# Seven block products in place of eight in a feed-forward part, as two phases through DRAM

## The chip, the cores and the metric

One core of one Trainium2 chip runs the whole program. The time is device time in microseconds; a kernel is run several times, and the median counts. The engines are TensorE (PE; its weight loads are PEld), VectorE (DVE), ScalarE (ACT), GpSimd (POOL) and SyncE (SP), which issues the DMAs. Each has its own queue of instructions, in an order that is fixed when the program is built.

## The reference

A trunk of two layers is run over 1024 latent tokens and 128 prompt tokens of width 1024. Each layer is norm, mixer (attention), gated residual, norm, feed-forward part, gated residual; the shifts, scales and gates come from a conditioning vector (one for the latent tokens, another for the prompt). The change is in the feed-forward part, of inner width D_FF = 2816 (22 tiles of 128):

```python
def conv_ffn(h, w_up, conv_w, conv_b, w_down):
    gate, val = jnp.split(h @ w_up, 2, axis=-1)
    gp = jnp.pad(gate, ((0, 0), (1, 1), (0, 0)))
    gate = gp[:, :-2] * conv_w[0] + gp[:, 1:-1] * conv_w[1] + gp[:, 2:] * conv_w[2] + conv_b
    return (jax.nn.silu(gate) * val) @ w_down
...
        x = x + g1 * o
        h = rmsnorm(x, W['g_ffn_norm'][l]) * (1 + sc2) + sh2
        x = x + g2 * conv_ffn(h, W['w_up'][l], W['conv_w'][l], W['conv_b'][l], W['w_down'][l])
```

## The kernel before

Features lie on partitions (8 tiles, KD), tokens in columns: 1152 tokens in 3 chunks of CW = 384, the last of which holds 256 latent tokens and the prompt. Every float32 operand is split into a high part (cast to fp32r on ACT) and a low part (the difference, on DVE): `split`, L82 and L83. A product is then three matmuls, high x high, high x low and low x high (`mm3`, L87 to L89). Each matmul loads its own 128x128 weights and streams the tokens of a chunk.

A layer ends with the output projection (`out_proj`: 8 output tiles x 3 chunks x 8 x 3 matmuls into `odps`, added to the residual stream x on DVE by `x_add`, L498; squares for the norm on ACT, L194, and summed on GpSimd, L195), the norm of each chunk (`norm_chunk`, which gives Hhi and Hlo), and `ffn`. For each of the 22 inner tiles f, `ffn` computes the gate (`fg`, 8 x 3 matmuls for each of 3 chunks), copies it out on ACT, does the width-3 convolution in three DVE operations (L581 to L583) and SiLU on ACT, computes the value (`fv`), multiplies and splits on DVE and ACT, and after every second f runs the down product of a finished pair (`fd`: 8 output tiles x 3 chunks x 2 x 3 matmuls, each group added to x at once, L498). The up and down weights of one load (128x1024, 512 KB) are split by one ACT and one DVE operation. x, the activations and the weights stay in SBUF; x is read from DRAM once, in layer 0.

In layer 0, the modulation of what comes later is computed behind this: in the output projection 8 column tiles on DVE (`mod_dve`, L115) and 8 on GpSimd and ACT (`mod_pool`, L132 and L133), in the feed-forward part 56 on DVE, in pieces of 512 columns, queued behind a convolution (`held`). GpSimd has almost nothing to do in the feed-forward part.

The code states dependencies only through tiles. A planner lays the instructions of each engine in order by the times that it assumes for them, so that instructions which are ready go ahead of earlier ones which wait; on the chip each engine then keeps that order. The code before and after is planned in the same way.

## Time and profile before

| what | value |
|---|---|
| runs | 3173.3 us median of 3 (3172.89 to 3174.28) |
| profiled execution, first to last instruction | 3174.0 us |
| PE busy | 3069.4 us (97%), 18557 matmuls |
| DVE busy | 2149.7 us (68%) |
| ACT busy | 1307.4 us (41%) |
| GpSimd busy | 817.8 us (26%) |
| DMA | 163.96 MB, mean 52 GB/s |

Matmuls are pipelined, so that PE's busy time doesn't tell how near it is to its limit; the distance between the starts of successive matmuls does. The recorded duration of a DVE operation holds some 0.08 us that overlaps the next one, so that the distance of starts is the better price there too.

### The profile page before, as it was taken

Reading aid. Unit: us, or ns where it says so; the run is one execution under the profiler, and the core shown is the slowest. Engines: PE = TensorE matmul, PEld = TensorE weight load, DVE = VectorE, ACT = ScalarE, POOL = GpSimd, SP = SyncE. Lnnn points to the kernel's source line nnn. Section 1 sums busy time; section 2 is a strip of 40 time slices with the busy share of each in tenths; the row PEclk is TensorE's granted clock in tenths of the full one; section 3 lists DMA queues with packets and bytes.
Section 4 is the critical chain, followed back from the end, with each engine's and each line's share of the span. In section 5 each row is a group of like instructions: output and inputs, shape, how many; then the busy total and the mean of one; then the engine's idle time right before and its main releaser. Section 6 shows DMA issues by size and latency. Waiting matters only on the chain.

```text
span 3174.0 us, 49141 instructions
## 1 busy us (share of the span) xinstructions
PE 3069.4 (97%) x18557; PEld 2936.0 (93%) x18557; DVE 2149.7 (68%) x4980; ACT 1307.4 (41%) x2608; POOL 817.8 (26%) x970
## 2 busy tenths in 40 slices
PE   8889999999979999999999998999999999999998
PEld 6778998889879999999999987988999999999997
DVE  6668997888778867776754766989364454444446
ACT  4428886777634121221111425998241211211112
POOL 4336762434272000000000404987220000000003
PEclk8989999999989999999999998999999999999999
DMA  6200000000332322222211110001110111111111
GB/s 227 73 21 1 1 14 14 5 3 15 128 132 71 117 86 87 80 88 87 85 47 40 34 40 13 2 2 34 34 47 34 42 50 43 40 47 40 41 40 60
DMA packets 63407, 163.96 MB, mean 52 GB/s; under 512 B 6481, under 2 KB 18529, under 8 KB 62913
## 3 DMA queue, kind: packets, MB, share of 16 engines
q1 hardware_dynamic: 62994, 160.41, 14.7%
q8 instruction: 146, 2.39, 0.3%
q14 instruction: 91, 0.75, 0.1%
q0 software_dynamic: 176, 0.41, 0.0%
HBM read 155.67 MB, written 5.13 MB: 51 GB/s over the span
## 4 chain that ended last, share of the span: by engine, by line
PE 83%; DVE 8%; ACT 3%; issue 3%; POOL 2%; DMA 2%; SPq 0%; DVEq 0%; ACTq 0%; POOLq 0%
PE sps L326 8%; PE fg L88 6%; PE fg L87 6%; PE fg L89 6%; PE fv L87 6%; PE fv L88 6%; PE fv L89 6%; PE fd L89 6%; PE fd L87 6%; PE ptps L371 6%; PE fd L88 6%; PE pvps L392 3%; PE pvps L391 3%; PE ips L87 1%; PE ips L89 1%
## 5 line engine op out<-in xcount | busy, mean ns | idle before, releaser
L498 DVE SCALAR_TENSOR_TENSOR x<-fd,mod,x 128x384 f32<-128x384 f32 (+1 forms) x704 | 345.2, 513 | 537.5 <-PE fd L89 536.3
L195 POOL TENSOR_TENSOR nacc<-nacc,nsq 128x384 f32<-128x384 f32 x75 | 90.3, 1205 | 1688.6 <-ACT nsq L194 1686.4
L82 ACT CAST whi<-wraw 128x1024 fp32r<-128x1024 f32 (+2 forms) x184 | 180.2, 981 | 521.3 <-PE fg L88 248.8
L89 PE MATMUL fd<-ahi,wlo 128*128 128x384 f32 x1056 | 357.0, 338 | 0.0
L88 PE MATMUL fd<-alo,whi 128*128 128x384 f32 x1056 | 355.2, 336 | 0.0
L87 PE MATMUL fd<-ahi,whi 128*128 128x384 f32 x1056 | 354.5, 337 | 0.3 <-DVE x L498 0.3
L87 PE MATMUL fg<-Hhi,whi 128*128 128x384 f32 x1056 | 354.0, 335 | 0.0
L88 PE MATMUL fg<-Hlo,whi 128*128 128x384 f32 x1056 | 354.0, 336 | 0.0
L89 PE MATMUL fg<-Hhi,wlo 128*128 128x384 f32 x1056 | 353.9, 335 | 0.0
L87 PE MATMUL fv<-Hhi,whi 128*128 128x384 f32 x1056 | 353.8, 335 | 0.0
L88 PE MATMUL fv<-Hlo,whi 128*128 128x384 f32 x1056 | 353.7, 335 | 0.0
L89 PE MATMUL fv<-Hhi,wlo 128*128 128x384 f32 x1056 | 353.5, 335 | 0.0
L315 POOL TENSOR_SCALAR prob<-prob,pm 128x1280 f32<-128x1280 f32 (+3 forms) x288 | 283.9, 994 | 211.9 <-DVE pm L348 191.9
L371 PE MATMUL ptps<-cst,prob 128*128 128x128 f32 x1920 | 293.7, 274 | 4.1 <-POOL prob L315 2.6
L83 DVE TENSOR_TENSOR wlo<-wraw,whi 128x1024 fp32r<-128x1024 f32 (+2 forms) x184 | 215.9, 1176 | 105.1 <-ACT whi L82 104.9
L83 DVE TENSOR_TENSOR ptlo<-ptps,pthi 128x512 fp32r<-128x512 f32 (+1 forms) x428 | 273.7, 654 | 12.8 <-ACT pthi L82 8.7
L82 ACT CAST pthi<-ptps 128x512 fp32r<-128x512 f32 (+1 forms) x428 | 232.6, 564 | 47.4 <-PE ptps L371 17.0
L332 DVE CUSTOM_DVE_ANT_0 prob<-sps,zero,pm 128x256 f32<-128x256 f32 (+1 forms) x384 | 217.8, 567 | 35.1 <-PE sps L326 20.2
L371 PEld LDWEIGHTS ptps<-cst,prob 128*128 128x128 f32 x1920 | 224.8, 141 | 15.0 <-POOL prob L315 7.0
L346 ACT ACTIVATE prob<-prob,pm 128x1280 f32<-128x1280 f32 (+1 forms) x144 | 181.5, 1262 | 47.2 <-DVE pm L332 45.2
L87 PEld LDWEIGHTS fd<-ahi,whi 128*128 128x128 f32 x1056 | 198.2, 188 | 1.3 <-issue 0.7
L89 PEld LDWEIGHTS fd<-ahi,wlo 128*128 128x128 f32 x1056 | 198.5, 188 | 0.0
(246 smaller groups left out, 7477.2 us busy)
## 6 DMA issues: line engine op xcount, KB each, us to landing
wraw<-w_up SPq DMA_DIRECT2D x88, 512.0 KB, 3.2
wm<-wmT SPq DMA_DIRECT2D x128, 256.0 KB, 2.6
wraw<-w_down SPq DMA_DIRECT2D x44, 512.0 KB, 3.3
x<-xT SPq DMA_DIRECT2D x6, 1536.0 KB, 12.1
wm<-wm SPq DMA_DIRECT2D x16, 512.0 KB, 7.1
wm<-wmT SPq DMA_DIRECT2D x16, 512.0 KB, 3.5
o_yT<-y SPq DMA_DIRECT2D x12, 384.0 KB, 2.8
wraw<-w_in_e SPq DMA_DIRECT2D x16, 256.0 KB, 3.0
```

The costliest lines, as they stand in the source:

```text
L82: self.nc.scalar.copy(hi, src)
L83: self.nc.vector.tensor_tensor(lo, src, hi.bitcast(F32), ALU.subtract)
L87: mm(out, ahi, bhi, start=first, stop=False)
L88: mm(out, ahi, blo, start=False, stop=False)
L89: mm(out, alo, bhi, start=False, stop=last)
L315: nc.gpsimd.tensor_scalar(p[:, :n], p[:, :n], r, 0.0, ALU.mult, ALU.add)
L326: nc.tensor.matmul(ps[:, :w], l, r[:, c0:c0 + w], start=(j == 0), stop=(j == np_ - 1))
L332: nc.vector.tensor_tensor_reduce(out=p[:, off:off + w], in0=ps[:, :w], in1=in1, scale=-g["scale"], scalar=init, op0=ALU.add, op1=ALU.min, ...
L346: nc.scalar.activation(p[:, :ne], p[:, :ne], AF.Exp, bias=m[:, i:i + 1], scale=-1.0, accum_out=m[:, 6:7])
L371: nc.tensor.transpose(pt[:, o:o + P], g["P"][u][:, kk * P:(kk + 1) * P], self.ident)
L391: nc.tensor.matmul(pv[:, :nu * P], v, hi[:, r], start=(kk == 0), stop=False)
L498: self.nc.vector.scalar_tensor_tensor(xs, d[:, s - c * CW:e - c * CW], self.mod[l][:, cond, gcol + m:gcol + m + 1], xs, ALU.mult, ALU.add)
```

## The change

The feed-forward products of both layers are rewritten as Winograd's form of Strassen's scheme: both operands are cut into 2 x 2 blocks (weights: two output tiles by two halves of the inner dimension; tokens: two halves of a chunk by the same two halves), sums and differences of blocks are formed, and 7 block products replace 8. Chunks are now 640 and 512 tokens, so that a block is 320 or 256 columns wide.

- Tokens: `combos` makes of four blocks seven operands, by four subtractions on GpSimd, and splits each into high and low parts (seven casts on ACT, seven subtractions on DVE). It runs in the norm (`norm_wino`: 4 times per chunk, one for each pair of feature tiles) and, in the down phase, for each of the 11 pairs of inner tiles and each chunk (`load`).
- Weights: `weights` reads the four blocks of a unit (1 MB in the up phase) into one buffer `wr`, forms four sums on GpSimd, and splits seven blocks on ACT and DVE into a ring of 5 (up) or 6 (down) places.
- `wino` runs the products of a unit in the order 1, 2, 6, 5, 7, 3, 4 on 3 kinds of PSUM banks. Products 1, 6, 7 and 4 go on summing in one bank, so that the bank is read between them.
- `up`: all gates and values of a layer. In a gate unit 4 of the 7 results are copied out on ACT and 3 added to on DVE; in a value unit 3 are copied on ACT, 3 added to on DVE, and the products with the gate are three on GpSimd and one on DVE for each chunk. The first convolution step moves from DVE to ACT. The activations go to DRAM (`acts`), but for the last pair. The first two units run for chunk 0 alone, then for chunk 1 alone; the others for both chunks.
- `down`: the activations come back pair by pair; a run is one i (output tiles i and i + 4) over up to three pairs, and its seven products are added to x by `gated_add` on DVE. The last pair's runs go by chunks.
- x no longer stays in SBUF: it is written to DRAM from the output projection and from the end of layer 0, and read again (`load_xt`) into space that other tiles had (the weight ring of the up phase has the space of x's chunk 0).
- Layer 1's input projection takes its weights into unused columns of the norm's tiles (`place`); its raw weights lie where the buffers of the feed-forward part lay.

The modulation behind the up phase stays on DVE, in the same 512-column pieces; the part on GpSimd is in 512 columns too.

```diff
+CH = ((0, 640), (640, 512))
+GW = T + 6
+VW = T + 4
...
+NPAIR = NF // 2
+PAIRS = (NPAIR - 1,) + tuple(range(NPAIR - 1))
...
+WINO = ((1, 0, "a"), (2, 1, "b"), (6, 5, "a"), (5, 4, "c"), (7, 6, "a"), (3, 2, "c"), (4, 3, "a"))
...
+        self.cvt = self.Fp.tile([P, 2560], F32, name="cvt", tag="cv")
+        self.gpt = self.Fp.tile([P, 2 * GW], F32, name="gpt", tag="gp")
+        self.tm = self.Fp.tile([P, 2304], F32, name="tmt", tag="tm")
+        self.wr = self.Fp.tile([P, 3072], F32, name="wrt", tag="wr")
...
+        return self.Bp.tile([P, 14 * h], F32R, name=f"B{c}", tag=f"B{c}", bufs=4)
...
+    def gated_add(self, l, c, m, off, n, src, gcol):
+        t0 = CH[c][0]
+        for s, e, cond in self.conds(t0 + off, t0 + off + n):
+            xs = self.xt[c][:, m, s - t0:e - t0]
+            self.nc.vector.scalar_tensor_tensor(xs, src[:, s - t0 - off:e - t0 - off],
                                                 self.mod[l][:, cond, gcol + m:gcol + m + 1], xs, ALU.mult, ALU.add)
...
+        (nc.vector if last else nc.gpsimd).tensor_tensor(acc, acc, t, ALU.add)
...
+    def combos(self, bt, c, b11, b12, b21, b22, on_pool=()):
+        nc = self.nc
+        def hl(j, src):
+            hi, lo, s = self.alike(self.slot(bt, c, 0, j), self.slot(bt, c, 1, j), src)
+            nc.scalar.copy(hi, s)
+            (nc.gpsimd if j in on_pool else nc.vector).tensor_tensor(lo, s, hi.bitcast(F32), ALU.subtract)
+        def sub(out, a, b):
+            nc.gpsimd.tensor_tensor(*self.alike(out, a, b), ALU.subtract)
+        hl(0, b11)
+        hl(1, b21)
+        sub(b11, b12, b11)
+        hl(2, b22)
+        sub(b12, b22, b12)
+        hl(4, b11)
+        sub(b22, b22, b11)
+        hl(5, b22)
+        hl(6, b12)
+        sub(b21, b21, b22)
+        hl(3, b21)
...
+    def norm_wino(self, c, ab):
+        nc = self.nc
+        a, b = ab
+        t0, w = CH[c]
+        h = w // 2
+        r = self.rstd2(c)
+        out = [self.btile(c) for kk in range(4)]
+        for kk in range(4):
+            hb = self.cvt[:, (kk % 2) * 2 * w:(kk % 2 + 1) * 2 * w].rearrange("p (a b) -> p a b", a=2)
+            for j in range(2):
+                k = kk + 4 * j
+                for s, e, cond in self.conds(t0, t0 + w):
+                    z = slice(s - t0, e - t0)
+                    nc.vector.scalar_tensor_tensor(hb[:, j, z], self.xt[c][:, k, z], a[:, cond, k:k + 1], r[:, z],
+                                                   ALU.mult, ALU.mult)
+                    nc.scalar.activation(hb[:, j, z], hb[:, j, z], AF.Identity, bias=b[:, cond, k:k + 1])
+            self.combos(out[kk], c, hb[:, 0, :h], hb[:, 0, h:], hb[:, 1, :h], hb[:, 1, h:])
...
+            parts = [(0, 320), (320, 320)] if c == 0 else [(0, 512)]
...
+                self.gated_add(l, c, m, off, n, d, 16)
+            self.square(c, m, sqb, m == 0, m == KD - 1)
+            nc.sync.dma_start(spill[:, m, t0:t0 + w], self.xt[c][:, m, :])
...
+        for m in range(M0, KD):
+            unit(m, 0)
+        H = [self.norm_wino(0, ab)]
+        for m in range(M0, KD):
+            unit(m, 1)
+        return H, lambda: H.append(self.norm_wino(1, ab))
...
+    def weights(self, units, slots):
+        nc = self.nc
+        i = 0
+        for src, n in units:
+            w = n * P
+            raw = self.wr[:, 0:4 * w].rearrange("p (a b) -> p a b", a=4)
+            nc.sync.dma_start(self.wr[:, 0:4 * w].rearrange("p (a n b) -> p a n b", a=4, b=P), src)
+            s1, s2 = self.wr[:, 4 * w:5 * w], self.wr[:, 5 * w:6 * w]
+            a11, a12, a21, a22 = (raw[:, j, :] for j in range(4))
+            sub = lambda o, x, y, op=ALU.subtract: nc.gpsimd.tensor_tensor(o, x, y, op)
+            sub(s1, a21, a22, ALU.add)
+            sub(s2, s1, a11)
+            sub(a21, a11, a21)
+            for prod, _, _ in WINO:
+                if prod == 3:
+                    sub(a12, a12, s2)
+                s = {1: a11, 2: a12, 6: s2, 5: s1, 7: a21, 3: a12, 4: a22}[prod]
+                t = slots(i % self.wring)
+                hi, lo = t[:, 0:w], t[:, w:2 * w]
+                self.split(hi, lo, s)
+                i += 1
+                yield hi, lo
...
+    def take(self):
+        want = self.wused + self.wring
+        while self.wmade is not None and len(self.wlist) < want:
+            n = next(self.wmade, None)
...
+    def wino(self, chunks, tiles, evac):
+        nc = self.nc
+        t = {c: {} for c in chunks}
+        for prod, j, s in WINO:
+            ahi, alo = self.take()
+            for c in chunks:
+                h = CH[c][1] // 2
+                new = prod in (1, 2, 5)
+                if new:
+                    t[c][s] = self.bank(s, "f" + s)
+                out = t[c][s][:, :h]
+                bs = tiles[c]
+                n = len(bs)
+                for kk in range(n):
+                    z = slice(kk * P, (kk + 1) * P)
+                    bhi, blo = (self.slot(bs[kk], c, zz, j) for zz in range(2))
+                    for i, (a, b) in enumerate(((ahi, bhi), (ahi, blo), (alo, bhi))):
+                        nc.tensor.matmul(out, a[:, z], b, start=new and kk == 0 and i == 0,
+                                         stop=kk == n - 1 and i == 2, skip_group_check=True)
+                evac(prod, c, {k: v[:, :h] for k, v in t[c].items()})
...
+        ring = self.Xp.tile([P, 5120], F32R, name="wring", tag="xa")
+        if arena:
+            arena()
+        bg = list(bg)
+        first = [(0, gv, (c,)) for c in range(2) for gv in range(2)]
+        units = first + [(p, gv, (0, 1)) for p in range(1, NPAIR) for gv in range(2)]
+        w_up = self.d["w_up"]
+        self.stream([(w_up[l, p, gv].rearrange("p a (n b) -> p a n b", b=P), 4) for p, gv, _ in units],
+                    lambda i: ring[:, i * 1024:(i + 1) * 1024], 5)
...
+        def conv(p):
+            n = T + 2
+            for f in range(2):
+                o = C_CONV + (l * NF + 2 * p + f) * 4
+                w = lambda i: self.cst[:, o + i:o + i + 1]
+                g = gpt[:, f * GW:(f + 1) * GW]
+                v = cv[:, f, :n]
+                nc.scalar.activation(v, g[:, 1:1 + n], AF.Identity, bias=w(3), scale=w(1))
+                nc.vector.scalar_tensor_tensor(v, g[:, 0:n], w(0), v, ALU.mult, ALU.add)
+                self.last_conv = nc.vector.scalar_tensor_tensor(v, g[:, 2:2 + n], w(2), v, ALU.mult, ALU.add).ins
+                nc.scalar.activation(v, v, AF.Silu)
...
+        for p, gv, cs in units:
+            if (p, gv, cs) == first[2]:
+                late_norm()
+                for f in range(2):
+                    for a, b in ((0, 1), (NS + 1, NS + 3), (T + 3, T + 4)):
+                        nc.gpsimd.memset(gpt[:, f * GW + a:f * GW + b], 0.0)
+            if gv == 0:
+                self.wino(cs, tiles(cs), gate)
+                if 1 in cs:
+                    conv(p)
+                    for f in later:
+                        f()
+                    later.clear()
+                    self.hold = {"dve": self.last_conv}
+                    n = -(-len(bg) // (NPAIR - p))
+                    for u in bg[:n]:
+                        u()
+                    del bg[:n]
+                continue
+            self.wino(cs, tiles(cs), val(1 not in cs))
+            if 1 in cs and p < NPAIR - 1:
+                nc.sync.dma_start(acts[p][:, :, 0:NS], cv[:, :, 0:NS])
+                nc.sync.dma_start(acts[p][:, :, NS:T], cv[:, :, NS + 2:T + 2])
...
+        runs = []
+        at = [0] * 4
+        for s in range(last):
+            for i in (0, 3, 1, 2):
+                if (s - i) % 3 == 0:
+                    runs.append((s, i, at[i], s))
+                    at[i] = s + 1
+        tail = [(last, i, at[i], last) for i in (1, 2, 0, 3)]
+        wd = self.d["w_down"]
+        seq = [(r, (0, 1)) for r in runs] + [(r, (c,)) for c in range(2) for r in tail]
+        rings = {}
+        def slots(i):
+            tag = "gp" if i < 3 else "cv"
+            if tag not in rings:
+                rings[tag] = self.Fp.tile([P, 3, 768], F32R, name="wr" + tag, tag=tag)
+            return rings[tag][:, i % 3, :]
+        self.stream([(wd[l, i][:, :, a:b + 1, :], b + 1 - a) for (s, i, a, b), _ in seq], slots, 6)
...
+        def load(q):
+            B[q] = []
+            for c, (t0, w) in enumerate(CH):
+                bt = self.btile(c)
+                B[q].append(bt)
+                h = w // 2
+                if q == 0:
+                    v = [self.tokens(self.cvt, f * VW, c, half) for f in range(2) for half in range(2)]
+                else:
+                    r = self.tm[:, 0:1280] if c == 0 else self.tm[:, 1280:2304]
+                    r = r.rearrange("p (a b) -> p a b", a=2)
+                    nc.sync.dma_start(r, acts[PAIRS[q]][:, :, t0:t0 + w])
+                    v = [r[:, f, half * h:(half + 1) * h] for f in range(2) for half in range(2)]
+                self.combos(bt, c, *v)
...
+        done = 0
+        for r, cs in seq[:len(runs)]:
+            while done < r[0]:
+                done += 1
+                load(done + 1)
+            run(r, cs)
+        if done < last - 1:
+            load(last)
...
+            for x, r in enumerate(tail):
+                run(r, (c,))
+                self.square(c, r[1], sqb[c], x == 0, False)
+                self.square(c, r[1] + 4, sqb[c], False, x == 3)
...
+    def load_xt(self, src):
+        self.xt = [self.Xp.tile([P, KD, w], F32, name=f"xt{c}", tag="xa" if c == 0 else "xb") for c, (t0, w) in enumerate(CH)]
+        for c, (t0, w) in enumerate(CH):
+            for m in range(0, KD, 2):
+                self.nc.sync.dma_start(self.xt[c][:, m:m + 2, :], src[:, m:m + 2, t0:t0 + w])
...
+        k.Xp = pl.open("X0", "right")
+        k.load_xt(d["xT"])
...
+    k.up(0, H, late0, acts[0], bg, None)
...
+        return k.norm_plain(c, abs_[0], [k.tm[:, 0:640], k.wr[:, 2304:2944]]), None
...
+    H = k.down(0, acts[0], xs_[0], after0)
...
+    k.rawp = pl.open("raw1", "left")
...
+        c, i = divmod(i, 12)
+        return k.spare(H[c][i // 3], c, i % 3)
+    put_q = lambda kk: (place(2 * kk), place(2 * kk + 1))
```

## Rows read from the trace of the kernel before

**Rows 1.** The page, chain that ended last: shares of the span by engine.
```profile
PE 83%; DVE 8%; ACT 3%; issue 3%; POOL 2%; DMA 2%; SPq 0%; DVEq 0%; ACTq 0%; POOLq 0%
```

**Rows 2.** Busy us by stage: window, length, engines (instructions), PE clock, DMA.
```profile
971.50:1802.60 831.10, 830.77 (x4784) 830.09 (x4784) 565.62 (x1156) 181.75 (x318) 29.08 (x31) 1.00 0.23 77
2216.00:2321.70 105.70, 105.65 (x600) 105.16 (x601) 44.91 (x69) 34.03 (x55) 23.89 (x22) 0.97 0.10 35
2321.70:3154.80 833.10, 833.10 (x4784) 832.78 (x4784) 415.47 (x704) 178.14 (x312) 29.48 (x33) 1.00 0.12 40
```

**Rows 3.** PE's timeline in an up product: start us, us, operation.
```profile
1300.65 0.33 PE L88 MATMUL fv<-Hlo,whi 128*128 128x384 f32 x1
...
1302.38 0.33 PE L89 MATMUL fv<-Hhi,wlo 128*128 128x384 f32 x1
```

**Rows 4.** PE's timeline, 512-wide and 256-wide input projection products.
```profile
1836.20 0.39 PE L88 MATMUL ips<-wlo,Hhi 128*128 128x512 f32 x1
...
1840.73 0.39 PE L87 MATMUL ips<-whi,Hhi 128*128 128x512 f32 x1
...
1867.92 0.28 PE L87 MATMUL ips<-whi,Hhi 128*128 128x256 f32 x1
...
1869.96 0.28 PE L89 MATMUL ips<-whi,Hlo 128*128 128x256 f32 x1
```

**Rows 5.** DVE's timeline around layer 0's output projection: start us, us, operation.
```profile
844.09 10.51 DVE L83 TENSOR_TENSOR olo<-o,ohi 128x768 fp32r<-128x768 f32 x12
...
867.98 0.61 DVE L498 SCALAR_TENSOR_TENSOR x<-odps,mod,x 128x384 f32<-128x384 f32 x1
868.51 2.89 DVE L83 TENSOR_TENSOR wlo<-wraw,whi 128x1024 fp32r<-128x1024 f32 x1
...
884.19 0.73 DVE L498 SCALAR_TENSOR_TENSOR x<-odps,mod,x 128x256 f32<-128x256 f32 x2
884.85 1.27 DVE L115 CUSTOM_DVE_ANT_0 mj<-wm,scb,cst 128x1024 bf16<-128x1024 f32 x1
```

**Rows 6.** GpSimd operations in mixer C by form: count | busy us, mean ns.
```profile
L378 POOL TENSOR_TENSOR ptlo<-ptf,pthi 128x512 fp32r<-128x512 f32 x30 | 38.7, 1288 | 2.0
...
L378 POOL TENSOR_TENSOR ptlo<-ptf,pthi 128x256 fp32r<-128x256 f32 x24 | 18.0, 750 | 0.2
```

**Rows 7.** DVE by form, 868 to 904 us.
```profile
L115 DVE CUSTOM_DVE_ANT_0 mj<-wm,scb,cst 128x1024 bf16<-128x1024 f32 x12 | 28.4, 2365 | 4.2 <-ACT scb L148 4.1
L83 DVE TENSOR_TENSOR wlo<-wraw,whi 128x1024 fp32r<-128x1024 f32 x2 | 4.9, 2468 | 0.0
```

**Rows 8.** GpSimd by form, 868 to 904 us.
```profile
L132 POOL TENSOR_TENSOR mpp<-wm,scb 128x1024 f32<-128x1024 f32 x8 | 25.5, 3200 | 32.7 <-DMA wm<-wmT 32.7
L195 POOL TENSOR_TENSOR nacc<-nacc,nsq 128x384 f32<-128x384 f32 x5 | 8.8, 1767 | 3.6 <-ACT nsq L194 3.6
```

**Rows 9.** DVE by form in layer 1's feed-forward part.
```profile
L83 DVE TENSOR_TENSOR wlo<-wraw,whi 128x1024 fp32r<-128x1024 f32 x62 | 75.9, 1224 | 50.5 <-ACT whi L82 50.4
...
L582 DVE SCALAR_TENSOR_TENSOR cv<-gp,cst,cv 128x1154 f32<-128x1154 f32 x22 | 31.2, 1417 | 0.4
```

**Rows 10.** DVE by form in layer 0, feed-forward part: modulation.
```profile
L115 DVE CUSTOM_DVE_ANT_0 mj<-wm,scb,mod 128x512 bf16<-128x512 f32 x112 | 83.5, 746 | 7.0 <-DMA wm<-wmT 6.1 <-DVE mod L115 0.2
```

**Rows 11.** Timeline at the end: from the last sum to the last scaling.
```profile
3161.22 1.44 PE L205 MATMUL nps<-cst,nacc 128*128 128x2 f32 x6 [5.62 <-DVE nacc L195]
...
3165.51 3.24 DVE L1185 SCALAR_TENSOR_TENSOR y<-x,cst,nps 128x384 f32<-128x384 f32 x6 [2.33 <-ACT npl L1178]
```

**Rows 12.** DMA issues: KB each, median us to landing.
```profile
wraw<-w_up SPq DMA_DIRECT2D x88, 512.0 KB, 3.2
```

**Rows 13.** PE's timeline behind a long wait: start us, us, operation.
```profile
948.67 1.14 PE L205 MATMUL nps<-cst,nacc 128*128 128x2 f32 x6 [4.68 <-DVE nacc L195]
...
950.13 0.52 PE L87 MATMUL odps<-ohi,whi 128*128 128x384 f32 x1
...
952.05 0.52 PE L87 MATMUL odps<-ohi,whi 128*128 128x384 f32 x1
```

More of the change, by code (lines that the diff above doesn't have):

```diff
@@ new lines, in bank, with conds, alike, tokens @@
+    def bank(self, tag, name):
+        return self.aps.tile([P, 512], F32, name=name, tag=tag, bufs=4 if tag == "a" else 2)
+    @staticmethod
+    def conds(a, b):
+        return [(s, e, i) for i, (s, e) in enumerate(((a, min(b, NS)), (max(a, NS), b))) if s < e]
+    @staticmethod
+    def alike(*aps):
+        if all(len(a.shape) == 2 for a in aps):
+            return aps
+        return [a.rearrange("p (a b) -> p a b", b=P) if len(a.shape) == 2 else a for a in aps]
+    @staticmethod
+    def tokens(flat, base, c, half):
+        t0, w = CH[c]
+        h = w // 2
+        a = base + t0 + half * h
+        if (c, half) == (1, 1):
+            return flat[:, a:a + 260].rearrange("p (a b) -> p a b", b=130)[:, :, 0:P]
+        return flat[:, a:a + h]
@@ L520, in out_proj @@
         bg = after_split() if after_split else []
+        sqb = [self.gpt[:, 0:640], self.gpt[:, 640:1280]]
         def unit(m, c):
[L523 to L529 removed]
@@ L530, in out_proj @@
-        M0 = KD - 3
+            t0, w = CH[c]
+            parts = [(0, 320), (320, 320)] if c == 0 else [(0, 512)]
+            for off, n in parts:
+                d = self.bank("a" if c == 0 else "b" if m >= M0 or m % 2 else "c", "odps")
+                for k in range(KD):
+                    h, l_ = ws[m][k // 4 * 2], ws[m][k // 4 * 2 + 1]
+                    z = slice((k % 4) * P, (k % 4 + 1) * P)
+                    ohi, olo = (self.plain(O[c][k % 4], c, zz, k // 4)[:, off:off + n] for zz in range(2))
+                    self.mm3(d[:, :n], h[:, z], l_[:, z], ohi, olo, k == 0, k == KD - 1)
+                self.gated_add(l, c, m, off, n, d, 16)
@@ L533, in out_proj @@
                 load(m)
-            for c in range(3):
+            for c in range(2):
                 unit(m, c)
@@ new lines, in take, with stream @@
+    def take(self):
+        want = self.wused + self.wring
+        while self.wmade is not None and len(self.wlist) < want:
+            n = next(self.wmade, None)
+            if n is None:
+                self.wmade = None
+            else:
+                self.wlist.append(n)
+        self.wused += 1
+        return self.wlist[self.wused - 1]
+    def stream(self, units, slots, ring):
+        self.wring, self.wused, self.wlist = ring, 0, []
+        self.wmade = self.weights(units, slots)
@@ new lines, in arena, with in_proj2 @@
+    def arena(self, scb, wmb, mpp=None):
+        self.scb2, self.wmb, self.mpp = scb, wmb, mpp
+        self.nc.sync.dma_start(scb.rearrange("p (a b) -> p a b", a=2), self.d["c_bc"])
+        self.nc.scalar.activation(scb, scb, AF.Silu)
+    def in_proj2(self, H, src, width, per, put, evac, after=None):
+        nc = self.nc
+        ws = {}
+        for g in range(KD // per):
+            n = per * width
+            raw = self.rawp.tile([P, 1024], F32, name="wraw2", tag="wraw2", bufs=2)
+            nc.sync.dma_start(raw[:, :n], src[g])
+            for i in range(per):
+                k = g * per + i
+                ws[k] = put(k)
+                self.split(*ws[k], raw[:, i * width:(i + 1) * width])
+        order = "abaca"
+        for tt in range(NTT):
+            c = 0 if tt < 5 else 1
+            cs = slice(tt * P - CH[c][0], (tt + 1) * P - CH[c][0])
+            ps = self.bank(order[tt % 5], "ips")
+            with (self.tc.issue_after(after[1]) if after and tt >= after[0] else nullcontext()):
+                for k in range(KD):
+                    hi, lo = (self.plain(H[c][k % 4], c, z, k // 4)[:, cs] for z in range(2))
+                    self.mm3(ps[:, :width], hi, lo, ws[k][0], ws[k][1], k == 0, k == KD - 1)
+            evac(tt, ps)
@@ L1193, in host_inputs @@
+        return None, last
+    k.down(1, acts[1], xs_[2], after1)
+    pl.close("ps2", "F2", "B2", "X1", "dram", "const")
 def host_inputs(x):
```

409 lines of the change are left out of this document (245 added, 164 removed).

## The prediction

> **What bounds the kernel now.** I read the chain of waits first: PE holds 83% of it [rows 1]. Then the stages: in both feed-forward parts (831.1 and 833.1 us) PE is busy without a gap at the full clock, while DVE is busy 566 and 415 us and GpSimd 29 us [rows 2]. So the matmuls' pitch is the price there, and the reader is to see two things: how the pitch falls with the width, and what DVE and GpSimd cost once they have to work together, which these stages don't show.
>
> **Pitch of PE.** Ten starts at 384 columns lie 1.73 us apart, 173 ns each [rows 3]; twenty at 512 take 4.53 us, 226.6 each; seventeen at 256 take 2.04 us, 120 each [rows 4]. That is N/2.4 + 13.3 ns at all three widths, so 146.6 at 320; between the measured 120 and 173 it can't be far off.
>
> **PE's gain.** Before: 2 layers x (3168 up + 1584 down) = 9504 matmuls x 173.3 = 1647.0 us. After: an up phase has 22 units x 7 products x 12 matmuls x 2 chunks = 3696, a down phase half of that, 1848; both layers 11088, half at 146.6 and half at 120: 1478.0. Gain 169.0 us, 84.5 a layer. The output projection keeps its columns (two 320 and one 512 cost 520 ns where three 384 cost 520).
>
> **Prices of the helpers.** DVE with two SBUF operands: 12 operations of 768 columns take 10.51 us, 0.876 each, N/0.96 + 76 ns. DVE reading PSUM: 384 columns take 0.53 from start to start (867.98 to 868.51), a pair of 256 and 128 takes 0.66 (884.19 to 884.85): N/0.96 + 130 [rows 5]. GpSimd with two operands: 1288 at 512, 750 at 256 [rows 6]: 2.10 N + 212 ns.
>
> **What GpSimd costs DVE.** Between 868 and 904 us both work on two-operand sums. DVE's 1024-column reductions take 2365 ns there [rows 7], 1.27 us alone (884.85 [rows 5]); its 1024-column subtraction takes 2468 ns [rows 7] against 1224 in the quiet feed-forward part [rows 9]. That is 12 x 1.09 + 2 x 1.24 = 15.6 us lost, some 17 with small ones, while GpSimd ran 8 of 1024 and 5 of 384 columns [rows 8], own time by the price above 8 x 2.36 + 5 x 1.02 = 24.0. So DVE lost about 0.72 of GpSimd's own time, with 83% of its own work on two-SBUF operations. The PSUM-reading additions (0.53) weren't slowed. The changed kernel puts both engines to such work all through the feed-forward part. I take 0.72 scaled by the share of two-SBUF work; the bounds are 0 (never at the same time) and 1 (each GpSimd operation holds DVE up for its whole length).
>
> The Trainium skill, "SBUF — State Buffer", section "SBUF: two separate sides", says that a DVE operation with two SBUF inputs and a GpSimd operation lock each other out for the whole instruction. By it the end of 1 is a limit that queues can really come to; what that gives stands among the rivals. The trace agrees in kind: 868.51 is 1.14 us of work in 2.89 us [rows 5].
>
> **Down phase, a layer.** PE 924 x (146.6 + 120) = 246.3. DVE: gated additions, 18 runs (counting a tail's two chunks as one) of 7 x 463 ns for chunk 0 and 3 x 397 + 8 x 263 for chunk 1, whose second half is cut at the prompt: 117.7; low parts of tokens, 11 x 7 x (409 + 343): 57.9; low parts of weights, 154 operations over 45,696 columns: 59.3. Sum 234.9, against PE's 246.3: DVE has no slack even undisturbed. GpSimd: 88 token differences (71.9), 88 weight sums over 26,112 columns x 2 (73.5), 14 squares (19.9): 165.3. Half of DVE's work is two-SBUF, so it loses 0.72 x 0.50/0.83 = 0.42 of that: 69. 304, and 2 for PE's start: 306, or 60 above PE. Most of it falls at the ends: the first runs span one pair, with 11 us of products for both runs against 16 us of DVE besides 20 for loading two pairs (10.5 its own, the rest lost to GpSimd's 13); in the tail each chunk has 18 to 22 us of products and some 28 of DVE. Bounds: 15 (the ends alone) and 154 (234.9 + 165.3). ACT, busy 182 of 831 us [rows 2], gets a cast for each low part and no more than that, and stays under DVE. Before, 11 x 8 such additions per layer lay beside a PE that was always behind them.
>
> **From the output projection to the up phase, a layer.** Before, the norms were hidden. Now, from the last product of chunk 0 to the first product that reads chunk 1's norm, PE has 3 units x 24 x 226.6 ns and 168 x 146.6 ns: 41 us. DVE has the norm of chunk 0 (8 x 743 + 28 x 409 ns = 17.4) and of chunk 1 (15.1), additions (2.4 + 2.8), low parts of two units of weights (8.5): 46; two waits for the reciprocal root at 4.3 us each (3161.22 to 3165.51 [rows 11]): 55; GpSimd has 14.1 + 12.0 + 10.3 + 3.9 = 40.3, of which DVE, on two-SBUF work nearly all the time, loses 0.75: 30. 85 less 5 that the first product needn't wait for, minus 41: PE stands still for 39. Bounds 9 and 60 (all of GpSimd, and the next two units, which have 30 us of DVE for 20 of PE).
>
> **Up phase else.** A pair has 44.8 us of PE. DVE: weights 8.5, additions and one product 6.0, convolution 4 x 1.34 [rows 9], 19.9; GpSimd 15.2. In layer 1 hidden beneath PE. In layer 0 the modulation adds 20.4 reductions of 0.75 [rows 10], DVE 35.2, plus 0.72 x 15.2 = 46.1: 1.3 over PE, ten pairs, about 10 us in all; bounds 0 and 50. A refill of `wr`, 1 MB, I estimate from 512 KB in 3.2 us [rows 12] at 6.4; the ring holds five products, 16 us for two chunks, which hides it and the first split (1.2). If it were not hidden, each us late is paid 40 times.
>
> **Smaller terms.** x's reload: 4.7 MB behind SP's queue, beside two units for each chunk whose banks wait (25 us): 0, bounds 0 and 15. Layer 1's input projection can't prefetch its weights, since their space is that of the last ring; four loads of 512 KB through two buffers, less what PE can do on the first: +10, bounds 0 and 20. The end, 512 columns in place of 384: +2, bounds -3 and +8. PE's clock: after a wait of 4.68 us six 384-column matmuls lie 0.32 us apart (950.13 to 952.05 [rows 13]), nearly twice 0.173, which is the 1.2 GHz level; eight or nine of them lose 1.3 us. Some four such waits a layer: +10, bounds 3 and 15.
>
> **Sum.** 3174.0 - 169.0 + 2 x 60 + 2 x 39 + 10 + 0 + 10 + 2 + 10 = 3235. The runs' median is 0.7 under the profiled span, so 3234 us, 2% slower. Its own range is 3175 to 3300: the loss is the difference of large sums.
>
> **Rivals.**
> *Faster: GpSimd hardly disturbs DVE.* The planner may lay GpSimd's sums beside PSUM additions, which speak for it by not being slowed. At a tenth of GpSimd's time, down is 234.9 + 16.5 with 12 for the ends, 17 above PE; the transition loses 13; modulation 0; the rest 14 (projection 8, end 1, clock 5): 3174 - 169 + 34 + 26 + 14 = 3079. Between, both losses grow with the fraction f of the down phase as 165 f - 9 and 9 + 72 f (the transition's fraction is 1.8 f): they eat a layer's 84.5, less 11 for half of the other terms, at f = 0.31. From there the kernel is slower. Against it: on 868 to 904 us the measured loss is far above.
>
> *Much slower: full alternation.* Every GpSimd sum holds DVE for its length: 2 x 154 + 2 x 49 + 50 + 27 - 169 = +314, 3488 us. Operations are shorter here than between 868 and 904 us, so DVE meets GpSimd more often; but half of its work in the down phase reads PSUM.
>
> *The weights come late.* One raw buffer and a ring of five: if a refill takes 21 us in place of 8, PE waits 5 us for each of 40 units, +200 on the forecast: 3434. The DMA is idle enough against it.
>
> *Narrow products gain nothing.* Recorded weight loads of 188 ns could be taken for a floor of 0.188 us; 11088 of them would take 438 us more than 1647. The 120 ns pitch at 256 columns, weights loaded for each, excludes that.
>
> **How the numbers follow.** Forecast family (3165 to 3315) 0.51, of which hardly any is within the bound; faster rival 0.34; within 0.2% (6 us, about what a measurement of this kernel can tell from no change) 0.06, which is f near 0.31; full alternation 0.05; late weights and the like 0.04. Faster 0.34, same 0.06, slower 0.60. The range reaches into the faster rival to 3100, leaving some 0.1 below, and to 3315, leaving about as much above.
>
> **What would show it.** Pitch 0.147 and 0.120 in the up phase (else PE's gain is wrong). Down phases near 306 us, DVE in them over 90% busy, its low-part subtractions longer than 0.42 us and PE waiting for DVE; near 260 with PE at 95% says that the faster rival holds. A gap of 30 us or more on PE in two places between the output projection and the second unit of chunk 1; the clock at half behind it. Up phases at 45 us a pair, in layer 0 slightly more. If the down phase is at PE's own time, or the gap under 15 us, the forecast fails in its sign.

## The result and the profile after

The changed kernel takes 3420.9 us (median of four runs, 3417.8 to 3424.6) against 3173.1 for the kernel before on the same chip: 1.078 times as long, 95% interval 1.077 to 1.080. The profiled execution spans 3420.1 us, and TensorE's mean granted clock fell from 0.982 to 0.929. The forecast was 3234, range 3100 to 3315: right in its sign, far off in its size.

Busy time by stage of the changed kernel, columns as in [rows 2]: projection and up phase of layer 0, its down phase, all that lies between, then projection, up and down phase of layer 1. An up or down phase runs here from its first product's start to its last one's.

```profile
845.10:986.20 141.10, 110.81 (x597) 99.54 (x597) 108.75 (x160) 64.03 (x134) 84.83 (x63) 0.89 0.42 148
986.20:1571.60 585.40, 527.19 (x3712) 513.72 (x3713) 504.19 (x860) 230.89 (x429) 246.74 (x185) 0.95 0.34 114
1571.60:1942.80 371.20, 298.70 (x1870) 279.02 (x1868) 331.64 (x664) 137.92 (x328) 186.31 (x185) 0.84 0.28 92
1942.80:2381.60 438.80, 397.37 (x2646) 355.12 (x2645) 325.80 (x1064) 289.22 (x682) 239.67 (x404) 0.94 0.06 19
2381.60:2503.90 122.30, 104.85 (x597) 96.09 (x597) 53.99 (x83) 39.42 (x67) 32.02 (x30) 0.92 0.31 112
2503.90:3041.00 537.10, 512.78 (x3713) 504.23 (x3714) 326.59 (x428) 229.62 (x429) 231.22 (x187) 0.96 0.20 72
3041.00:3400.40 359.40, 291.75 (x1869) 276.93 (x1868) 317.00 (x634) 132.04 (x320) 184.43 (x187) 0.87 0.26 85
```

In [rows 2] PE had no gap in either feed-forward part and the clock stood at 1.00. Now no phase is without gaps. The matmuls alone would need 492.8 us for an up phase and 246.3 for a down phase, so the four phases lose 92.6, 124.9, 44.3 and 113.1 us. Of these 375 us, 152 are extra busy time of PE (527.2 - 492.8, 298.7 - 246.3, 512.8 - 492.8, 291.8 - 246.3), which goes with the lower clock (0.84 to 0.96, where it was 1.00); 223 are waits.

The pitch itself is as forecast. In the body of layer 1's up phase, where PE hardly waits, 3506 recorded matmuls keep PE busy for 471.74 us, 134.5 ns each at a clock of 0.99; the forecast, answering to [rows 3, 4], was the mean of 146.6 and 120, 133.3.

```profile
2560.00:3041.00 481.00, 471.74 (x3506) 468.82 (x3507) 279.88 (x360) 200.79 (x361) 202.89 (x163) 0.99 0.21 76
```

What PE waits for in the body of layer 0's up phase, and what DVE waits for (us in total, times, longest):

```profile
PE fa L786 <- DVE gpt L809: 21.7, 11, 3.0
PE fa L786 <- DVE tmt L809: 7.3, 7, 2.3
...
DVE wring L92 <- ACT wring L91: 56.5, 18, 5.8
```

PE waits for additions of DVE (L809), while DVE stands idle for 56.5 us in front of low parts of weights (L92). One such place on DVE's timeline (start us, us, operation), with SP's, GpSimd's and PE's behind it:

```profile
1193.72 0.69 DVE L92 TENSOR_TENSOR wring<-wrt,wring 128x512 fp32r<-128x512 f32 x1
1194.32 0.75 DVE L1008 CUSTOM_DVE_ANT_0 junk<-arena,mod 128x512 bf16<-128x512 f32 x1
...
1200.64 2.94 DVE L92 TENSOR_TENSOR wring<-wrt,wring 128x512 fp32r<-128x512 f32 x2 [5.57 <-ACT wring L91]
1203.51 0.81 DVE L809 TENSOR_TENSOR gpt<-gpt,fa 128x320 f32<-128x320 f32 x2
1204.24 1.03 DVE L92 TENSOR_TENSOR wring<-wrt,wring 128x512 fp32r<-128x512 f32 x1
...
1194.43 0.33 SPq L735 DMA_DIRECT2D wrt<-w_up  x1
...
1200.07 6.34 POOL L738 TENSOR_TENSOR wrt<-wrt 128x512 f32<-128x512 f32 x4 [13.37 <-DMA wrt<-w_up]
...
1204.04 3.38 PE L786 MATMUL fa<-B,wring 128*128 128x320 f32 x16 [2.66 <-DVE gpt L809]
```

The reader is to see an order. The last low part of a unit (1193.72) frees the raw buffer, SP issues the next transfer at 1194.43, and DVE's next operation but one (a reduction, with its readout, comes between) is a low part out of just that transfer. DVE stands there for 5.57 us, with two additions queued behind it whose PSUM bank PE wants: PE waits 2.66 us for them. By the time the low parts can run, GpSimd's four sums have begun, and two low parts take 2.94 us, where 2 x 0.61 is their own time by my price.

In layer 1's down phase DVE is busy for 317.0 of 359.4 us. Its operations by form (count | busy us, mean ns), first of the changed kernel, then of one without GpSimd's sums (e1):

```profile
L612 DVE TENSOR_TENSOR B<-tmt,B 128x320 fp32r<-128x320 f32 x70 | 49.7, 725 | 0.7 <-ACT B L611 0.7
L566 DVE SCALAR_TENSOR_TENSOR xt<-fa,mod,xt 128x320 f32<-128x320 f32 x72 | 38.6, 540 | 8.7 <-PE fa L786 8.5
L92 DVE TENSOR_TENSOR wrgp<-wrt,wrgp 128x384 fp32r<-128x384 f32 x46 | 37.5, 822 | 5.3 <-ACT wrgp L91 5.3
```
```profile
L566 DVE SCALAR_TENSOR_TENSOR xt<-fa,mod,xt 128x320 f32<-128x320 f32 x72 | 39.2, 544 | 12.9 <-PE fa L786 12.5
L612 DVE TENSOR_TENSOR B<-tmt,B 128x320 fp32r<-128x320 f32 x70 | 30.6, 481 | 0.9 <-ACT B L611 0.9
...
L92 DVE TENSOR_TENSOR wrgp<-wrt,wrgp 128x384 fp32r<-128x384 f32 x46 | 24.4, 550 | 8.3 <-ACT wrgp L91 8.2
```

Beside the sums, low parts with two SBUF operands take 725 for 481 and 822 for 550 ns; the additions that read PSUM take 540 and 544, undisturbed. Of the 42 us in which DVE is idle, 35 go to these waits:

```profile
DVE xt L566 <- PE fa L786: 15.7, 22, 1.3
DVE wrgp L92 <- ACT wrgp L91: 10.6, 10, 2.5
DVE wrcv L92 <- ACT wrcv L91: 8.8, 8, 1.6
```

ACT's casts in turn wait for the weights, 58.0 us in all, and for GpSimd's sums of tokens:

```profile
ACT B L611 <- POOL tmt L615: 40.0, 63, 2.3
ACT wrcv L91 <- DMA wrt<-w_down: 30.9, 9, 7.3
ACT wrgp L91 <- DMA wrt<-w_down: 27.1, 8, 4.9
```

### The profile page after: what moved, and what is told of

Read it like the earlier page. It is cut to its first block, busy times and chain, and to the rows that moved or that the text cites. A ratio compares the mean times of both kernels' runs of the same rounds, so it can differ in the third digit from the quotient of the medians.

```text
span 3420.1 us, 55665 instructions
## 1 busy us (share of the span) xinstructions
PE 3037.5 (89%) x20141; PEld 2829.2 (83%) x20141; DVE 2658.7 (78%) x5754; ACT 1690.2 (49%) x3538; POOL 1596.8 (47%) x1656
## 5 line engine op out<-in xcount | busy, mean ns | idle before, releaser
L738 POOL TENSOR_TENSOR wrt<-wrt 128x512 f32<-128x512 f32 (+3 forms) x368 | 471.0, 1296 | 659.8 <-DMA wrt<-w_up 400.2
L786 PE MATMUL fa<-B,wring 128*128 128x256 f32 (+1 forms) x4224 | 623.2, 304 | 102.3 <-ACT wring L91 42.5
L786 PEld LDWEIGHTS fa<-B,wring 128*128 128x128 f32 x4224 | 593.7, 195 | 118.5 <-ACT wring L91 44.7
L92 DVE TENSOR_TENSOR wring<-wrt,wring 128x512 fp32r<-128x512 f32 x336 | 351.4, 1061 | 205.5 <-ACT wring L91 202.3
L91 ACT CAST wring<-wrt 128x512 fp32r<-128x512 f32 x336 | 200.0, 617 | 370.9 <-DMA wrt<-w_up 106.2
L786 PE MATMUL fc<-B,wring 128*128 128x320 f32 (+1 forms) x2112 | 305.8, 298 | 11.2 <-DVE wring L92 5.6
L786 PEld LDWEIGHTS fc<-B,wring 128*128 128x128 f32 x2112 | 291.4, 191 | 15.6 <-DVE B L612 8.0
L92 DVE TENSOR_TENSOR ptlo<-ptps,pthi 128x512 fp32r<-128x512 f32 (+1 forms) x428 | 274.0, 654 | 14.6 <-ACT pthi L91 10.2
L786 PE MATMUL fa<-B,wrgp 128*128 128x320 f32 (+1 forms) x1074 | 188.0, 322 | 43.4 <-DVE xt L566 18.7
L786 PE MATMUL fa<-B,wrcv 128*128 128x320 f32 (+1 forms) x1038 | 181.4, 322 | 37.4 <-DVE xt L566 25.1
L335 PE MATMUL sps<-kh,qT 128*128 128x384 f32 (+3 forms) x472 | 175.5, 376 | 6.4 <-DVE pm L341 3.7
```

The lines of the kernel that those rows point to most:

```text
L91: self.nc.scalar.copy(hi, src)
L92: self.nc.vector.tensor_tensor(lo, src, hi.bitcast(F32), ALU.subtract)
L335: nc.tensor.matmul(ps[:, :w], l, r[:, c0:c0 + w], start=(j == 0), stop=(j == np_ - 1))
L738: sub = lambda o, x, y, op=ALU.subtract: nc.gpsimd.tensor_tensor(o, x, y, op)
L786: nc.tensor.matmul(out, a[:, z], b, start=new and kk == 0 and i == 0, stop=kk == n - 1 and i == 2, skip_group_check=True)
```

## The experiments

All are the changed kernel with an edit, of which the lines that matter are shown; phase lengths in us as above, "own" is the matmuls' time by the forecast's pitch. e3 is in the text alone.

| kernel | total | up 0 | down 0 | up 1 | down 1 | DVE busy in down 1 |
|---|---|---|---|---|---|---|
| own | | 492.8 | 246.3 | 492.8 | 246.3 | |
| after | 3420.9 | 585.4 | 371.2 | 537.1 | 359.4 | 317.0 |
| e1 no sums | 3218.1 | 513.9 | 324.3 | 513.2 | 315.0 | 253.3 |
| e2 no low parts | 3187.9 | 518.5 | 299.0 | 515.8 | 294.5 | 146.8 |
| e6 neither | 3167.2 | 513.9 | 298.2 | 510.1 | 290.5 | 146.1 |
| e5 no loads | 3294.4 | 533.6 | 338.8 | 525.5 | 325.7 | 309.9 |
| e11 neither, no loads | 3115.8 | 510.6 | 270.5 | 505.7 | 265.6 | 144.1 |
| e8 sums on DVE | 3330.8 | 548.3 | 349.4 | 524.6 | 341.2 | 314.7 |
| e9 and later splits | 3324.7 | 546.6 | 348.4 | 524.6 | 337.0 | 314.4 |
| e4 down in eight | 3301.0 | 583.9 | 309.5 | 537.3 | 300.0 | 140.8 |
| e10 mixed | 3244.8 | 552.2 | 304.2 | 527.6 | 282.4 | 137.3 |
| e12 second raw buffer | 3213.6 | 521.6 | 304.0 | 518.9 | 294.6 | 140.7 |
| e7 useless products | 3434.2 | 583.9 | 376.9 | 536.7 | 372.1 | 318.6 |

**e1, no block sums.**

```
 def sub(out, a, b):
-    nc.gpsimd.tensor_tensor(*self.alike(out, a, b), ALU.subtract)
+    return
...
-sub = lambda o, x, y, op=ALU.subtract: nc.gpsimd.tensor_tensor(o, x, y, op)
+sub = lambda o, x, y, op=ALU.subtract: None
```

> Leaves out all block sums on GpSimd in the feed-forward part (of weights and of tokens; the raw blocks stand in their place). My theory: DVE, held up by GpSimd, sets the pace wherever PE waits, and PE's half clock follows from the waits. Down phases then take about 300 us (layer 0, with the norm in its tail) and 275 (layer 1) in place of 397 and 359, the two stretches from the output projection to the full-width products 60 in place of 74, layer 0's up phase some 30 less: 3180 us, 240 less than the changed kernel. Rival: DVE's own work and the single buffers set the pace, and GpSimd's sums only take the 63 us a down phase by which DVE's low parts are longer than their own time, half of it hidden: 3330 or more. Second rival, weights late from DRAM: within 20 us of 3420.

3218.1 us. The rival (3330 or more) is out; the sums were worth 203 us where I had put 240, and the down phases came to 324.3 and 315.0 us for the 300 and 275 of my theory. DVE's busy time in layer 1's down phase fell by 63.7 us (317.0 to 253.3).

**e2, no low parts.**

```
-(nc.gpsimd if j in on_pool else nc.vector).tensor_tensor(lo, s, hi.bitcast(F32), ALU.subtract)
...
-hi, lo = t[:, 0:w], t[:, w:2 * w]
-self.split(hi, lo, s)
+hi = lo = t[:, 0:w]
+nc.scalar.copy(hi, s)
...
```

> Leaves out DVE's low parts of weights and tokens in the feed-forward part (the high part stands in their place, so PE has the same products), GpSimd's sums stay. If DVE's occupancy sets the pace: it loses 117 us of its own and some 60 of disturbance in each down phase, which then take 290 (layer 0) and 270 us; the up phases lose 40 and 25 us: about 3165 us. If what PE waits for is GpSimd's chain of sums, or the weights' arrival: 3330 or more.

3187.9 us, near the first. GpSimd still makes all its sums, so these alone don't hold PE up. The edit also takes the low part out of the chain that frees the raw buffer, so it can't tell DVE's occupancy from that chain. And DVE is now busy half of the time, yet the down phases still lose 53 and 48 us.

**e6, neither.** The edits of e1 and e2 together.

> Leaves out both the block sums and the low parts (raw blocks and high parts in their place); products, loads, casts and additions stay. Shows what is left of the loss when DVE and GpSimd have next to nothing to do. If DVE and GpSimd are the whole cause: down phases at 260 us (the last additions and PE's start), the stretch from the output projection to full-width products within 10 us of PE's time: about 3080 us. If the separate phases lose by their form (short runs at both ends, a transfer behind each of them): down phases at 285 to 295 as without low parts alone, and 3130 to 3150 us.

3167.2 us, level with the kernel before (ratio 0.997, 0.996 to 0.999). That is beyond both ranges, nearest to the second. Here my theory fell short on its other side: without the sums and the low parts (DVE is busy for 146 of 290.5 us in layer 1's down phase), all but some 7 us of the products' gain of 169 is still gone. Beside e2 it also shows that GpSimd's sums cost 21 us when DVE has slack; e1 put them at 203 when it has none.

**e5, no loads, and e11, neither and no loads.**

```
-nc.sync.dma_start(self.wr[:, 0:4 * w].rearrange(...), src)
+if i == 0:
+    nc.sync.dma_start(self.wr[:, 0:4 * w].rearrange(...), src)
```

> Leaves out all loads of feed-forward weights but each phase's first (the raw buffer keeps what stood in it), so that no unit waits for a transfer; all sums, casts, low parts and products stay. If the chain of a weight unit (raw buffer free only after the last unit's last low part, then the transfer, then three sums, then casts) makes DVE and PE wait: each down phase loses the some 40 us in which DVE stands idle, the up phase of layer 0 some 30: about 3310 us. If DVE's and GpSimd's occupancy alone sets the pace: within 20 us of 3420.

3294.4 us: 126 us less, as the first theory said. Layer 0's up phase:

```profile
983.20:1516.80 533.60, 510.56 (x3713) 502.73 (x3713) 503.67 (x862) 230.40 (x429) 259.06 (x185) 0.96 0.25 81
```

DVE is as busy in this up phase as before the edit (503.7 and 504.2), in 52 us less: they were DVE's waits for weights. But such a wait needn't cost PE time. In e1, which has the loads and not the sums, DVE stands nearly as long in the body of this phase, and the phase takes 513.9 us all the same, 21 over its own time:

```profile
DVE wring L92 <- ACT wring L91: 48.7, 12, 6.0
```

Loads and sums cost together: the waits hurt where DVE has no slack to make up for them.

> Leaves out block sums, low parts and all loads of feed-forward weights but each phase's first: products, casts, additions and evacuations stay. Of the 162 us that stand between the kernel without sums and low parts (3167) and the products' own time (3174 - 169 = 3005), this tells the weights' arrival from the form of the phases. If it is the arrival: down phases at 260 in place of 298 and 291, up phases at 500: 3090 us or less. If it is the form (the gap of 17 us behind the output projection, short runs at the ends): 3140 or more.

3115.8 us, between the two. The middles of layer 0's up and down phases in e11:

```profile
1030.00:1440.00 410.00, 410.00 (x3105) 410.00 (x3105) 265.30 (x566) 172.77 (x306) 66.41 (x58) 1.00 0.28 89
1530.00:1700.00 170.00, 170.00 (x1277) 170.00 (x1276) 78.47 (x183) 67.81 (x169) 0.00 (x0) 1.00 0.14 43
```

PE has no gap there, and the granted clock is 1.00. So, taken away in this order, of the 416 us between 3005 (3174 less 169) and 3421 sums and low parts hold 254, the weights' arrival 51, and the form of separate phases 111: what lies around their ends and between them. The order matters, since loads and sums cost together: taken away first, the loads are worth 126. Two examples of the form are the start of layer 1's up phase, where after the last product of the projection PE waits 17.4 us for the first weights, and the start of layer 1's input projection, where it waits 18.5 us for its first weights (before, PE's longest wait there was 0.9). Both stand in the changed kernel; e11 still has 11.8 and 18.4 of them, and e12 has 16.2 of the first.

```profile
PE fa L786 <- ACT wring L91: 17.6, 2, 17.4
PE ips L96 <- ACT B L91: 18.5, 1, 18.5
```

The ring shares its space with x of chunk 0, and the first split starts at 2503.23, just behind the norm's last read of that chunk (2500.99, 1.48 us). That the shared space is the cause is read from the code and these times; no run moves the ring.

**e8, sums on DVE.**

```
-nc.gpsimd.tensor_tensor(*self.alike(out, a, b), ALU.subtract)
+nc.vector.tensor_tensor(*self.alike(out, a, b), ALU.subtract)
...
-sub = lambda o, x, y, op=ALU.subtract: nc.gpsimd.tensor_tensor(o, x, y, op)
+sub = lambda o, x, y, op=ALU.subtract: nc.vector.tensor_tensor(o, x, y, op)
```

> All block sums on DVE in place of GpSimd. By my price the 88 sums of tokens and 88 of weights in a down phase take DVE 33 + 34 us of its own, where GpSimd's took 64 from it by disturbance: DVE is as busy as before, and the chain is shorter (0.41 for 1.0 us a sum): 3400 us, 25 up or down. If GpSimd is of real help (its sums lie beside DVE's PSUM additions): DVE gets 67 us more in each down phase and some 54 in each up phase: 3550 or more.

3330.8 us, 90 less than with GpSimd, better than either theory had it. DVE's busy time came out as expected: 314.7 us in layer 1's down phase, where it had been 317.0 with GpSimd doing the sums. GpSimd took from DVE what the sums cost on DVE itself. A sum of weights on GpSimd (changed kernel) and on DVE (e8), in that phase:

```profile
L738 POOL TENSOR_TENSOR wrt<-wrt 128x384 f32<-128x384 f32 x52 | 61.4, 1198 | 80.8 <-DMA wrt<-w_down 57.7 <-DVE xt L566 20.9 <-DVE wrgp L92 0.6
L738 DVE TENSOR_TENSOR wrt<-wrt 128x384 f32<-128x384 f32 x52 | 28.2, 558 | 6.2 <-DMA wrt<-w_down 6.2
```

With 1198 for 558 ns a sum, the chain behind each transfer is longer on GpSimd. That this is what the 90 us come from is argued and not isolated.

**e3 and e7, useless products where PE waits.** They write into unused columns of a bank that holds running sums, and change these sums.

```
+self.nc.tensor.matmul(self.fbank[:, 384:512], self.identr, self.identr, start=True, stop=True, skip_group_check=True)
```

> Adds products without use (128x128, into unused columns of the last PSUM bank) where PE waits: 10 ahead of each product of a down phase's first two runs, 6 ahead of each of its last eight, 180 ahead of the first product of an up phase. They are some 100 us of PE's time in waits of 261. If half clock itself is what takes PE's 156 extra busy us, the clock rises and the time falls by 60 to 100, to 3320 to 3360 us. If DVE's pace sets these stretches and half clock only stretches matmuls into time that PE would wait anyway: the clock in them rises just the same, PE's waits grow, and the time stays at 3420, 15 up or down.

3481.5 us, which neither theory foresaw: they took about twice the time that I had reckoned and were more than the waits that they were put into. e7 has fewer:

> Useless 128x128 products as before but fewer (4 ahead of each product of the first two runs of a down phase, 2 ahead of each of the last eight, 130 ahead of an up phase; each took 0.13 us at full clock, so 15 + 15 + 17 us a layer, under the waits that stand there). If half clock costs time by itself: 3370 or less. If DVE's pace sets these stretches: 3420 to 3440.

3434.2 us, in the range of the second theory. But the edit doesn't test it. Layer 1 in e7: the projection with the useless products behind it, then the first products of the up phase; last the same first products of the changed kernel:

```profile
2381.40:2503.20 121.80, 118.78 (x726) 110.31 (x726) 54.07 (x83) 39.36 (x67) 32.13 (x30) 0.98 0.32 113
2503.20:2507.00 3.80, 2.77 (x9) 2.35 (x10) 3.80 (x5) 3.80 (x10) 3.80 (x4) 0.50 0.00 0
2503.90:2507.70 3.80, 2.78 (x9) 2.36 (x10) 3.80 (x5) 3.80 (x10) 3.80 (x4) 0.50 0.00 0
```

In the first stretch the clock rose from 0.92 to 0.98, as the useless products fill 14.35 of the 17.4 us at full clock. Behind them 3.03 us of waiting are left, and the first products of the up phase run at 0.50 (1.2 GHz) in both kernels. So the products behind the wait never had the full clock, and that the two stretches took 658.5 us in place of 659.4 says nothing of its price. In the down phases the clock hardly moved (0.87 and 0.86 for 0.84 and 0.87). What half clock costs stays open.

**e9, transfer issued earlier and splits later.** On e8: the next unit's transfer right behind the last split, its splits two products later.

```
+for _ in range(LATER if u else 0):
+    yield None
...
+if prod == WINO[-1][0]:
+    fetch(u + 1)
```

> Block sums on DVE, and each weight unit's transfer issued right behind the last low part of the unit before it, its splits two products later, so that DVE isn't queued behind weights that are on their way. If the late weights hurt by DVE standing in its order in front of PE's additions: of the 126 us that the missing loads were worth about half comes back, most of it in layer 0's up phase: 3331 - 60 = 3270 us. If only the transfer's place matters (one raw buffer): within 15 us of 3331.

3324.7 us, within the range of the second theory. But the edit hardly changed what it was to change. In the body of layer 0's up phase DVE, which now makes the sums, stands in front of weights on their way nearly as long as in e8; e8 first, then e9:

```profile
DVE wrt L738 <- DMA wrt<-w_up: 35.4, 16, 3.8
DVE wrt L745 <- DMA wrt<-w_up: 29.5, 16, 4.4
```

In that body DVE has, but for a handful, the same operations in the same order in both; the planner lays them by the times that it assumes. So e9 doesn't decide between the transfer's place and DVE's order.

**e4, down phase in eight products.**

```
-self.wino(cs, {c: [B[q][c] for q in range(a, b + 1)] for c in cs}, evac(i))
+self.eight(cs, {c: [B[q][c] for q in range(a, b + 1)] for c in cs}, evac(i))
```

> The up phase alone in seven products; the down phase, still apart and through DRAM, in eight products without block sums (320 and 512 columns wide: 1584 products of 146.6, 146.6 and 226.6 ns a layer over three, 274.5 us), DVE then at some 126 us a layer. If the seven products' helpers are what down phases lose on: they take about 300 (layer 0, with the norm) and 285 us: 3250 us. If the separate phase itself loses (reload of x, loading of two pairs, last runs of one chunk): 340 and 320, and 3325 us.

3301.0 us, between the two. The down phases take 309.5 and 300.0, less than in seven, though their products need 274.5 in place of 246.3. Without sums DVE is busy for half of the time, and 25 to 35 us are still lost. In layer 1 most of that is the weights' arrival: with two raw buffers (e10, where some weights of the last runs are overwritten) its down phase takes 282.4. Layer 0's still takes 304.2 there.

**e10 and e12, mixed.** e12 adds to up in seven and down in eight a second raw buffer in the up phases. In e10 the second raw buffer of the down phase shares space with the squares of the final norm, so that some weights of the last runs are overwritten; in e12 the last eight runs use one.

```
+if u < 3 or u % 2 == 0:
+    where[u] = ("wr", self.wr[:, 0:2048])
+else:
+    where[u] = ("raw2", self.raw2)
```

> Up phase in seven products with sums on DVE and late splits, down phase in eight products with two raw buffers, modulation of layer 1's last 8 columns moved to layer 1's up phase. By the parts: 3301 for the eight-product down phase, less 37 + 13 (sums on DVE in the up phases), 30 (late splits), 15 (two raw buffers), 15 (modulation): 3190 us, still not under the kernel before. If the parts overlap, as they hide behind the same waits: 3220 to 3240.

3244.8 us, 5 above the second range: the parts overlap.

> The up phase in seven products with its block sums on DVE, made in place in the raw blocks, and a second raw buffer for the weights in both up phases (from the fourth unit on); the down phase in eight products with two raw buffers except in its last eight runs; modulation of layer 1's last 8 columns in layer 1's up phase. If late weights are what holds DVE, and so PE, in the up phases: layer 0's 552 us come to 515 and layer 1's 528 to 512, 3245 - 50 = 3195 us. If DVE's own work in layer 0 (some 470 us of 552) sets that phase: within 15 us of 3245.

3213.6 us (ratio 1.012, 1.010 to 1.014): three fifths of the expected gain. The up phases came from 552.2 to 521.6 and from 527.6 to 518.9, while layer 1's down phase, whose last eight runs are back at one buffer, went from 282.4 to 294.6. In the body of layer 0's up phase DVE's waits for weights, e10 first, then e12:

```profile
DVE wrt L745 <- DMA wrt<-w_up: 50.1, 17, 7.7
DVE wring L93 <- ACT wring L92: 8.3, 15, 1.6
```

The second buffer takes most of these waits away; the sums in place and the moved modulation buffers changed with it and aren't told apart. It is 6% faster than the changed kernel, but no version here that does the whole work beats the kernel before.

## Why the prediction was wrong

- **PE's gain** (169.0) held: 134.5 ns for 133.3. The feed-forward parts before took 1664.2 us together [rows 2] and not 1647.0, so that the losses stage by stage add up to 17 us more than the 416 above.
- **What GpSimd costs DVE** held. I had DVE lose 69 us in a down phase, 0.42 of GpSimd's time; e1 gives 63.7, with GpSimd's sums at about 145 us by my price, 0.44. Low parts with two SBUF operands went from 481 ns without the sums to 725 beside them, additions that read PSUM from 544 to 540. The Trainium skill, "SBUF — State Buffer", section "SBUF: two separate sides", has the lock held, on DVE's side, by an operation with two SBUF inputs or in a two-port mode; the trace agrees as to the two inputs. Two figures of this part of the sum are slightly off, without weight: 17 of 24.0 is 0.71 and not 0.72, and the 73.5 us of the weight sums go by 26,112 columns once, not twice.
- **The down phase at 306 us** is the step that failed. Its DVE time was right: 304 forecast, 317.0 measured in layer 1, of which some 11 are the final norm. The error was to set the phase's length equal to it. The phase took 359.4 us, since DVE was also idle for 42: 3 us of the first 69, 19 of the next 210 and 20 of the last 80, half of it behind PE's products (15.7 and some 4 us), half behind weights. Layer 0's took 371.2. Forecast over PE's own time 2 x 60, measured 124.9 + 113.1.

```profile
3041.00:3110.00 69.00, 47.83 (x255) 43.76 (x254) 66.05 (x143) 28.20 (x77) 38.13 (x43) 0.73 0.41 141
3110.00:3320.00 210.00, 191.01 (x1377) 187.47 (x1376) 190.92 (x377) 78.23 (x182) 107.53 (x104) 0.98 0.24 75
3320.00:3400.00 80.00, 52.52 (x240) 45.29 (x238) 60.03 (x115) 25.61 (x61) 38.39 (x39) 0.70 0.18 63
```

- **The refill that "the ring holds ... which hides"** failed with it. The transfer's size was right or better (1 MB landed in 4.8 us, for my 6.4), and the ring did cover it for PE, which itself waits only some 9 us for weights in the body of layer 0's up phase. What I left out is DVE's order: the first low part of the new unit comes two operations behind the one that frees the buffer, and DVE waits there with PE's additions behind it, 56.5 us in that body. This is read from the timeline and from e5 and e12; no run changes the order alone. e5 puts all loads at 126 us, with the sums in place; without sums and low parts they are worth 51. The rival "the weights come late" had nearly the total (3434), at a chance of 0.04, but by luck: it had PE waiting 5 us for each of 40 units, where DVE waits 18 times, 3.1 us on the mean, and it left the helpers as forecast.

```profile
wrt<-w_up SPq DMA_DIRECT2D x48, 1024.0 KB, 4.8
```

- **From projection to up phase**, with layer 0's up phase: 2 x 39 + 10 forecast. Against the projections of the kernel before (105.7 us in layer 1 [rows 2], 127.4 in layer 0, 844.11 to 971.50) and PE's own time, layer 1 lost 61 us (122.3 + 537.1 - 105.7 - 492.8) and layer 0 106 (141.1 + 585.4 - 127.4 - 492.8). e6, without sums and low parts, leaves 28 in each, which no term of the sum held; the wait of 17.4 us for the first weights is the largest piece that the trace of the changed kernel shows there.
- **Clock at half** (10 us): PE's busy time grew by 152 us. No run gives the products behind a wait the full clock, so how much of this is on the way, and how much only fills time in which PE would wait anyway, stays open.
- **Layer 1's input projection** (+10): 413.4 us from the end of the feed-forward part to the output projection became 438.8, +25, and one wait of 18.5 us for its first weights is most of that: the term was sized too small. **The end** (+2): 19.7 us for 19.2.
- **The rivals.** "GpSimd hardly disturbs DVE" and "narrow products gain nothing" are out by the rows above: DVE lost 0.44 of GpSimd's time and not a tenth, and a product takes 134.5 ns and not 188. "Full alternation" had the size nearly (3488) but not the cause: DVE lost 0.44 of GpSimd's time, not all of it.

As a sum: helpers forecast at 208 (2 x 60 + 2 x 39 + 10), measured at 254; form of the phases and weights' arrival forecast at 22 (the three small terms of 10, 10 and 2), measured at 162, in the order in which e6 and e11 take them away.

## What to carry to other kernels

When two phases that were interleaved are separated, price each phase's first and last runs and every refill in the order of each engine's queue, not by busy time: an engine that is 88% busy can't be the bound for its busy time alone. A helper's work given to GpSimd isn't free for DVE where DVE has no slack; here doing it on DVE left DVE just as busy and the kernel 90 us faster. One buffer between a transfer and an engine that works in order was here a wait on that engine (50.1 us in one phase, 8.3 with a second buffer), though a ring of five products stood behind it; and such a wait costs most where the engine has no slack.

## What was not expected of the hardware

A useless product of 128 columns is hardly cheaper than one of 256: 127 in a row took 14.35 us, 113 ns each, in e7 at a granted clock of 1.00, against 120 at 256 columns [rows 4]. N/2.4 + 13.3 ns, which held at 256, 384 and 512 columns [rows 3, 4] and at 320 in the changed kernel (twelve starts in 1.76 us, 2516.76 to 2518.52, 146.7 each), would give 67.

```profile
2485.83 14.35 PE L774 MATMUL odps<-identr 128*128 128x128 f32 x127
```
